# Weight sums of the first two feed-forward tiles on another engine, one shared slot, and a later place for the finishing of rows 0 to 3, in a transformer layer on one core

## The chip, the cores and the metric

The kernel runs on one core of a Trainium2 chip. The metric is the device time of one execution in microseconds, lower is better; several runs are given with their median.

## The reference, cut to what matters

One encoder layer: a mixing block with two attentions, a cross attention to 256 memory tokens, a SwiGLU feed-forward block, and a last RMSNorm. Sequence 1024, width 1024, inner width of the feed-forward block 2816, all float32. The change touches the feed-forward block and the last norm only:

```python
def rmsnorm(x, g):
    xf = x.astype(jnp.float32)
    y = xf * lax.rsqrt(jnp.mean(xf * xf, axis=-1, keepdims=True) + EPS)
    return (y * g.astype(jnp.float32)).astype(x.dtype)

def swiglu(h, w_gate_up, w_down):
    g, u = jnp.split(h @ w_gate_up, 2, axis=-1)
    return (jax.nn.silu(g) * u) @ w_down
...
        hf = rmsnorm(x, norm_ffn_g[layer])
        x = x + swiglu(hf, w_gate_up[layer], w_down[layer])
    return rmsnorm(x, norm_final_g)
```

## The kernel before, in words

Every product is a float32 product made of three matmuls on operands that are split into a high part (a cast on ScalarE, L896) and a low part (a subtraction on VectorE, L897): high by high, low by high, high by low (L902, L903, L904). The feed-forward block is class FeedForward. Both of its matrix products are done with seven sub-products instead of eight (a Strassen scheme), numbered 1 to 7 and taken in the order 1, 2, 6, 5, 7, 3, 4.

**First product (gate and up).** It goes over 11 tiles of 2 x 128 columns; Tile2 with f = 0 is here called tile 0, with f = 2 tile 1. Each tile has two pairs of weight blocks, g (gate) and u (up). A step of the list `items` is one sub-product of one pair: 12 matmuls of 128x512. The first 18 steps are: 1 g, 1 u, 2 g, 2 u of tile 0, the same four of tile 1, and then 6, 5, 7, 3, 4 (g and u each) of tile 0; steps 18 to 27 are 6, 5, 7, 3, 4 of tile 1. From tile 2 on, all seven follow one another.

- The weights of a pair are loaded into a tile `fr` with blocks a11, a12, a21, a22. Sub-products 6, 5, 7 and 3 need sums of blocks. Pair.make makes them in place on GpSimd, L956, L957, L958 (before 6) and L960 (before 3), each a tensor_tensor of 128x512. The sum s1 has a slot of its own of the kind "sum". make then splits the block into `w`. make is called four steps ahead (AHEAD).
- The activations (transposed, `hq`) are summed and split for each sub-product on VectorE and ScalarE by mov_late (L925, L927, L930, L935, then L897 into `T`); it is called in steps 2, 7, 9 and 11 for the sub-products 6 and 5, 7, 3 and 4.
- Pair.read takes results out of PSUM into rows `r`: L990 is the copy that opens a row (after 1, 6 and 5), L992 the addition of a later one. A PSUM bank of sub-product 1 takes 6 on top of it, so 6 of a pair cannot start before the copy after 1 of the same pair. What follows the products 1 and 2 of tile 1 is put off to step 15 (`later`).
- The slots: "sum" is a pool of two (tag raw), used for r of every u pair after sub-product 1 and for s1; "four" is a pool of eight (tag t2, 128x2048). Tile 1's g pair takes its row in half of a "four", its u pair in a "sum".
- At the end of sub-product 3 the gate row of tile 0 is multiplied by its up row (L1030, on VectorE for tile 0), which is the last use of u's row.

**Second product (down).** 77 steps, 11 for each of the seven sub-products, four row blocks (tt) of 12 matmuls / 4 each. down_make splits the operands two steps ahead into `do`; the last four go into other slots ("hidden"). `dr` are the loads, in a ring of eight: the load eight steps ahead waits for the split of the step that frees its slot, and stands in SyncE's queue in order. Sub-product 3 ends rows 0 to 3, sub-product 4 rows 4 to 7: add adds the PSUM bank (L1157), ScalarE takes squares (L1151), GpSimd makes the norm's factor (L1162 to L1164), and finish(row) scales both halves (L1145, VectorE) and sends them out (L1147, SyncE). Steps 72 to 76 of the list are done last, row block by row block.

The order of the instructions on each engine is drawn up at build time by a scheduler that takes the order of the code as priority and its own durations. `keep_in_program_order` (around L1145) pins an instruction behind the one that the code wrote before it on the same engine; nothing is pinned behind it. Each engine then works its list in order.

Of the kernel before, what the change touches and what calls it, by code (L numbers as in the profile page):

```python
# [12 lines left out]
ALU = mybir.AluOpType  # L13
# [10 lines left out]
FT = DFF // P  # L24
# [842 lines left out]
class FeedForward:  # L867
# [70 lines left out]
    class Pair:  # L938
# [11 lines left out]

        def make(self, n, w, s1):
            (a11, a12), (a21, a22) = ([self.raw[:, i, :HALF], self.raw[:, i, HALF:]] for i in range(2))
            pool, sub = self.ff.pool, ALU.subtract
            if n == 6:
                self.s1 = s1
                pool.tensor_tensor(out=s1, in0=a21, in1=a22, op=ALU.add)  # L956
                pool.tensor_tensor(out=a21, in0=a11, in1=a21, op=sub)  # L957
                pool.tensor_tensor(out=a11, in0=s1, in1=a11, op=sub)  # L958
            if n == 3:
                pool.tensor_tensor(out=a12, in0=a12, in1=a11, op=sub)  # L960
            src = {1: a11, 2: a12, 6: a11, 7: a21, 3: a12, 4: a22}[n] if n != 5 else self.s1
            self.w[n] = w
            self.ff.split(w[:, 0], w[:, 1], src)
# [13 lines left out]
        def read(self, n):  # L977
            ff = self.ff
            acc = self.bk[ff.BANK[n]]
            if n == 1:  # L980
                tile = ff.tiles["four"]("r")[:, :2] if self.f == 2 else ff.tiles["sum" if self.f >= FT else "row"]("r")
                self.r = [tile, None]
            elif n == 5:
                self.r[1] = ff.tiles["row"]("r")

            to = {1: (0, 0), 2: (0, 0), 6: (0, 1), 3: (0, 1), 5: (1, 1), 7: (1, 1)}.get(n)
            if to:
                r = self.r[to[0]][:, to[1]]
                if n in (1, 6, 5):
                    ff.act.copy(out=r, in_=acc)  # L990
                else:
                    ff.dve.tensor_tensor(out=r, in0=r, in1=acc, op=ALU.add)  # L992
# [139 lines left out]
    def down(self):  # L1132
        act, dve, pool, sp = self.act, self.dve, self.pool, self.sp
        LOADS, MADE, LAST = 8, 2, 5
        for i in range(4, LOADS):
            self.down_load(i)
        self.down_make(1)
        xs = []
        sf = self.cst.tile([P, NT, 2], F32, name="sf")
        bks = {}  # L1140
        fin = []

        def finish(row):
            for c in range(2):
                self.tc.keep_in_program_order(dve.scalar_tensor_tensor(  # L1145
                    out=xs[row][:, c], in0=xs[row][:, c], scalar=sf[:, row, 1:2], in1=gbc[:, c], op0=ALU.mult, op1=ALU.mult))
                sp.dma_start(out=self.out[row * P:(row + 1) * P, c * HALF:(c + 1) * HALF], in_=xs[row][:, c])  # L1147

        def squares(row, c):
            o = self.tiles["sum"]("fin")  # L1150
            act.activation(o[:, c], xs[row][:, c], AF.Square, accum_out=sf[:, row, c:c + 1])  # L1151

        def add(n, tt):
            b = "a" if self.BANK[n] == "a" else "c"
            half, c = {1: (0, 0), 2: (0, 0), 6: (0, 1), 5: (1, 1), 7: (1, 1), 3: (0, 1), 4: (1, 0)}[n]
            row = half * 4 + tt
            dve.tensor_tensor(out=xs[row][:, c], in0=xs[row][:, c], in1=bks[b][tt], op=ALU.add)  # L1157
            if n in (2, 7, 3, 4):
                squares(row, c)
            if n in (3, 4):  # L1160
                s0, s1 = sf[:, row, 0:1], sf[:, row, 1:2]
                pool.tensor_tensor(out=s1, in0=s0, in1=s1, op=ALU.add)  # L1162
                pool.tensor_scalar(out=s1, in0=s1, scalar1=1.0 / D, scalar2=EPS, op0=ALU.mult, op1=ALU.add)
                pool.tensor_tensor(out=s1, in0=s1, in1=self.mhalf, op=ALU.pow)  # L1164
                fin.append(row)
                if tt:
                    finish(fin[-2])
                if tt == 3:
                    finish(fin[-1])

        def mm(n, j, tt):
            bk = bks["a" if self.BANK[n] == "a" else "c"][tt]
            hi, lo = self.ops[self.ORDER.index(n) * (FT // 2) + j]
            ts = slice(tt * P, (tt + 1) * P)
            first = n in self.FIRST
            self.prod(bk, (hi[:, 0, ts], lo[:, 0, ts]), (hi[:, 1], lo[:, 1]), first and j == 0, j == FT // 2 - 1, not first)

        for i, (n, j) in enumerate(self.steps):
            if i >= len(self.steps) - LAST:
                break  # L1180
            self.down_load(i + LOADS)
            self.down_make(i + MADE)
            if i == 4:
                for x_d in self.x_d:
                    t = self.tiles["pair"]("xr")
                    sp.dma_start(out=t, in_=x_d)
                    xs += [t[:, k].rearrange("p (a b) -> p a b", a=2) for k in range(2)]
                gbc = self.tiles["row"]("gbc")
                sp.dma_start(out=gbc, in_=self.g_final.partition_broadcast(P).rearrange("p (a b) -> p a b", a=2))
            if n in self.FIRST and j == 0:  # L1190
                bks["a" if self.BANK[n] == "a" else "c"] = [self.bank() for _ in range(4)]
            for tt in range(4):
                mm(n, j, tt)
            if j == FT // 2 - 1:
                for tt in range(4):
                    add(n, tt)

        for k in range(i + MADE, len(self.steps)):
            self.down_make(k)
        for tt in range(4):  # L1200
            for n, j in self.steps[i:]:
                mm(n, j, tt)
            add(n, tt)
# [59 lines left out]
```

## Time and profile before

| what | us |
|---|---|
| median of 3 runs (lowest, highest) | 1790.8 (1789.49, 1791.02) |
| the profiled execution, its own time | 1787.65 |
| span of the profiled execution | 1785.8 |
| TensorE's mean granted clock, as a share of full speed | 0.997 |

All times in rows are from the start of the span of this one execution. The feed-forward block's first product starts at 1140.8, its second one at 1565. A row of the timeline gives start, duration, engine, line, operation, output and inputs, count of merged instructions, and in brackets how long the engine had been idle and what ended the idle time.

### The profile page before, as it was taken

Reading aid. Unit: us, or ns where it says so; the run is one execution under the profiler, and the core shown is the slowest. Engines: PE = TensorE matmul, PEld = TensorE weight load, DVE = VectorE, ACT = ScalarE, POOL = GpSimd, SP = SyncE. Lnnn points to the kernel's source line nnn. Section 1 sums busy time; section 2 is a strip of 40 time slices with the busy share of each in tenths; the row PEclk is TensorE's granted clock in tenths of the full one; section 3 lists DMA queues with packets and bytes.
Section 4 is the critical chain, followed back from the end, with each engine's and each line's share of the span. In section 5 each row is a group of like instructions: output and inputs, shape, how many; then the busy total and the mean of one; then the engine's idle time right before and its main releaser. Section 6 shows DMA issues by size and latency. Waiting matters only on the chain.

```text
span 1785.8 us, 23577 instructions
## 1 busy us (share of the span) xinstructions
PE 1743.1 (98%) x8836; PEld 1469.2 (82%) x8836; DVE 1085.4 (61%) x1497; ACT 765.6 (43%) x1425; POOL 516.0 (29%) x553
## 2 busy tenths in 40 slices
PE   7999999999999999999999999999999999999997
PEld 7778797898898888888888887778888888888886
DVE  6585666656766644435645545886676656655556
ACT  5354554545545544213542334453333333334343
POOL 3231213213323201200000001476766655400002
PEclk9999999999999999999999999999999999999999
DMA  5331313212222256412331113315645434587664
GB/s 193 103 93 66 102 47 104 65 60 61 68 85 63 76 195 233 156 62 86 116 118 49 58 59 135 125 71 195 253 163 191 165 142 174 215 283 193 195 192 139
DMA packets 75729, 229.79 MB, mean 129 GB/s; under 512 B 9184, under 2 KB 9440, under 8 KB 71776
## 3 DMA queue, kind: packets, MB, share of 16 engines
q1 hardware_dynamic: 75616, 228.30, 37.8%
q8 instruction: 69, 1.13, 0.3%
q14 instruction: 44, 0.36, 0.1%
HBM read 160.10 MB, written 55.57 MB: 121 GB/s over the span
## 4 chain that ended last, share of the span: by engine, by line
PE 65%; issue 3%; DVE 3%; ACT 1%; POOL 1%; DMA 1%; DVEq 0%; POOLq 0%; ACTq 0%
PE bk L903 11%; PE bk L904 11%; PE bk L902 11%; PE acc L217 5%; PE acc L218 5%; PE acc L219 5%; PE s L96 2%; PE s L95 2%; PE s L97 2%; PE s L217 2%; PE s L218 2%; PE s L219 2%; PE av L454 1%; PE tr L438 1%; PE av L95 0%
## 5 line engine op out<-in xcount | busy, mean ns | idle before, releaser
L218 PE MATMUL acc<-t,wsp 128*128 128x512 f32 (+1 forms) x704 | 270.5, 384 | 0.0
L217 PE MATMUL acc<-t,wsp 128*128 128x512 f32 (+1 forms) x704 | 270.5, 384 | 0.0
L219 PE MATMUL acc<-t,wsp 128*128 128x512 f32 (+1 forms) x704 | 270.4, 384 | 0.0
L902 PE MATMUL bk<-T,w 128*128 128x512 f32 x616 | 240.0, 390 | 2.2 <-ACT r L990 2.0
L903 PE MATMUL bk<-T,w 128*128 128x512 f32 x616 | 239.8, 389 | 1.3 <-DVE w L897 1.3
L904 PE MATMUL bk<-T,w 128*128 128x512 f32 x616 | 239.8, 389 | 0.4 <-DVE T L897 0.4
L897 DVE TENSOR_TENSOR w<-fr,w 128x512 fp32r<-128x512 f32 x132 | 142.9, 1115 | 69.5 <-ACT w L896 69.1
L81 DVE TENSOR_TENSOR wsp<-raw,wsp 128x1024 fp32r<-128x1024 f32 x98 | 122.1, 1246 | 74.1 <-ACT wsp L76 72.9
L76 ACT CAST wsp<-raw 128x1024 fp32r<-128x1024 f32 x96 | 100.7, 1049 | 124.8 <-PE s L219 50.2
L219 PEld LDWEIGHTS acc<-t,wsp 128*128 128x128 f32 x704 | 133.3, 189 | 25.2
L218 PEld LDWEIGHTS acc<-t,wsp 128*128 128x128 f32 x704 | 133.3, 189 | 23.0 <-DVE wsp L81 0.8
L217 PEld LDWEIGHTS acc<-t,wsp 128*128 128x128 f32 x704 | 133.3, 189 | 22.2
L897 DVE TENSOR_TENSOR do<-dr,do 128x1024 fp32r<-128x1024 f32 x77 | 96.5, 1260 | 78.3 <-ACT do L896 76.1
L902 PEld LDWEIGHTS bk<-T,w 128*128 128x128 f32 x616 | 115.6, 188 | 26.6 <-ACT r L990 2.4
L903 PEld LDWEIGHTS bk<-T,w 128*128 128x128 f32 x616 | 115.6, 188 | 25.5 <-DVE w L897 1.7
L904 PEld LDWEIGHTS bk<-T,w 128*128 128x128 f32 x616 | 115.6, 188 | 25.0 <-DVE T L897 0.9
L896 ACT CAST do<-dr 128x1024 fp32r<-128x1024 f32 x77 | 81.0, 1053 | 112.6 <-PE bk L904 98.6
L903 PE MATMUL bk<-do 128*128 128x512 f32 x308 | 120.0, 390 | 2.5 <-DVE do L897 2.5
L904 PE MATMUL bk<-do 128*128 128x512 f32 x308 | 119.8, 389 | 0.0
L217 PE MATMUL acc<-wsp,t 128*128 128x256 f32 (+1 forms) x368 | 118.3, 321 | 1.0 <-POOL wsp L80 1.0
L902 PE MATMUL bk<-do 128*128 128x512 f32 x308 | 119.0, 389 | 0.0
L219 PE MATMUL acc<-wsp,t 128*128 128x256 f32 (+1 forms) x368 | 116.8, 318 | 0.7 <-DVE wsp L81 0.7
(218 smaller groups left out, 3728.9 us busy)
## 6 DMA issues: line engine op xcount, KB each, us to landing
fr<-in_wgu SPq DMA_DIRECT2D x44, 512.0 KB, 5.3
ad<-r SPq DMA_DIRECT2D x22, 512.0 KB, 3.3
sd<-s SPq DMA_DIRECT2D x11, 1024.0 KB, 4.1
dw<-in_wdn SPq DMA_DIRECT2D x22, 512.0 KB, 5.4
wd<-dw SPq DMA_DIRECT2D x11, 1024.0 KB, 3.9
dr<-sd SPq DMA_DIRECT2D x44, 256.0 KB, 3.7
dr<-wd SPq DMA_DIRECT2D x44, 256.0 KB, 3.9
dr<-ad SPq DMA_DIRECT2D x33, 256.0 KB, 5.0
```

The source lines that it names most:

```text
L76: act.copy(out=hi, in_=src)
L81: lo_eng.tensor_tensor(out=lo, in0=src, in1=hi.bitcast(F32), op=ALU.subtract)
L95: pe.matmul(acc, lh, rh, start=(i == 0), stop=False)
L96: pe.matmul(acc, ll, rh, start=False, stop=False)
L217: pe.matmul(acc, lh, rh, start=(i == 0), stop=False)
L218: pe.matmul(acc, ll, rh, start=False, stop=False)
L219: pe.matmul(acc, lh, rl, start=False, stop=(i == n - 1))
L896: self.act.copy(out=hi, in_=src)
L897: self.dve.tensor_tensor(out=lo, in0=src, in1=hi.bitcast(F32), op=ALU.subtract)
L902: mm(acc, l[0], r[0], start=start, stop=False, skip_group_check=onto)
L903: mm(acc, l[1], r[0], start=False, stop=False, skip_group_check=onto)
L904: mm(acc, l[0], r[1], start=False, stop=stop, skip_group_check=onto)
```

## The change

The four kinds of weight sums of tiles 0 and 1 (both pairs) are issued on VectorE in place of GpSimd. The u pair of tile 1 takes its row in the second half of the "four" slot of its g pair, in place of a "sum" slot. The rows 0 to 3 are no longer finished at the end of sub-product 3, but one each after the steps j = 1, 2, 3, 4 of sub-product 4, the last one. Rows 4 to 7 are finished as before.

```diff
         def make(self, n, w, s1):
             (a11, a12), (a21, a22) = ([self.raw[:, i, :HALF], self.raw[:, i, HALF:]] for i in range(2))
-            pool, sub = self.ff.pool, ALU.subtract
+            sub = ALU.subtract
+            eng = self.ff.pool if self.f % FT >= 4 else self.ff.dve
             if n == 6:
                 self.s1 = s1
-                pool.tensor_tensor(out=s1, in0=a21, in1=a22, op=ALU.add)
-                pool.tensor_tensor(out=a21, in0=a11, in1=a21, op=sub)
-                pool.tensor_tensor(out=a11, in0=s1, in1=a11, op=sub)
+                eng.tensor_tensor(out=s1, in0=a21, in1=a22, op=ALU.add)
+                eng.tensor_tensor(out=a21, in0=a11, in1=a21, op=sub)
+                eng.tensor_tensor(out=a11, in0=s1, in1=a11, op=sub)
             if n == 3:
-                pool.tensor_tensor(out=a12, in0=a12, in1=a11, op=sub)
+                eng.tensor_tensor(out=a12, in0=a12, in1=a11, op=sub)
...
             if n == 1:
-                tile = ff.tiles["four"]("r")[:, :2] if self.f == 2 else ff.tiles["sum" if self.f >= FT else "row"]("r")
-                self.r = [tile, None]
+                if self.f % FT == 2:
+                    if self.f < FT:
+                        ff.second = ff.tiles["four"]("r")
+                    i = self.f // FT * 2
+                    self.r = [ff.second[:, i:i + 2], None]
+                else:
+                    self.r = [ff.tiles["sum" if self.f >= FT else "row"]("r"), None]
...
-        fin = []
...
-                fin.append(row)
-                if tt:
-                    finish(fin[-2])
-                if tt == 3:
-                    finish(fin[-1])
+                if n == 4 and tt:
+                    finish(row - 1)
+                if row == 7:
+                    finish(row)
...
             for tt in range(4):
                 mm(n, j, tt)
+            if n == 4 and j in (1, 2, 3, 4):
+                finish(j - 1)
```

## Rows read from the trace of the kernel before

**Rows 1.** The page's first part: busy time of each engine, share, instructions.
```profile
PE 1743.1 (98%) x8836; PEld 1469.2 (82%) x8836; DVE 1085.4 (61%) x1497; ACT 765.6 (43%) x1425; POOL 516.0 (29%) x553
```
**Rows 2.** TensorE's timeline from 1160: matmuls before which it sat idle.
```profile
1165.30 0.50 PE L903 MATMUL bk<-T,w 128*128 128x512 f32 x1 [1.27 <-DVE w L897]
...
1167.64 0.50 PE L904 MATMUL bk<-T,w 128*128 128x512 f32 x1 [0.45 <-DVE T L897]
...
1197.99 0.50 PE L902 MATMUL bk<-T,w 128*128 128x512 f32 x1 [1.96 <-ACT r L990]
...
1753.38 0.50 PE L903 MATMUL bk<-do 128*128 128x512 f32 x1 [2.03 <-DVE do L897]
...
1756.65 0.50 PE L903 MATMUL bk<-do 128*128 128x512 f32 x1 [0.48 <-DVE do L897]
```
**Rows 3.** GpSimd's timeline, 1143 to 1189: the weight sums of tiles 0 and 1.
```profile
1143.45 3.52 POOL L956 TENSOR_TENSOR s<-fr 128x512 f32<-128x512 f32 x2
...
1154.39 3.96 POOL L960 TENSOR_TENSOR fr<-fr 128x512 f32<-128x512 f32 x2
...
1170.60 13.72 POOL L956 TENSOR_TENSOR s<-fr 128x512 f32<-128x512 f32 x1 [12.25 <-ACT w L896]
...
1185.52 2.99 POOL L957 TENSOR_TENSOR fr<-fr 128x512 f32<-128x512 f32 x2
```
**Rows 4.** VectorE's timeline, 1138 to 1168.
```profile
1138.84 1.88 DVE L897 TENSOR_TENSOR w<-fr,w 128x512 fp32r<-128x512 f32 x3
...
1147.51 0.69 DVE L794 COPY hq<-bk 128x512 f32<-128x512 f32 x1 [1.68 <-PE bk L791]
1148.11 1.22 DVE L925 TENSOR_TENSOR hq<-hq 128x1024 f32<-128x1024 f32 x1
1149.75 1.28 DVE L897 TENSOR_TENSOR w<-fr,w 128x512 fp32r<-128x512 f32 x1 [0.42 <-ACT w L896]
1150.96 2.31 DVE L925 TENSOR_TENSOR hq<-hq 128x1024 f32<-128x1024 f32 x1
...
1155.43 1.77 DVE L897 TENSOR_TENSOR w<-fr,w 128x512 fp32r<-128x512 f32 x1
1157.12 2.31 DVE L927 TENSOR_TENSOR hq<-hq 128x1024 f32<-128x1024 f32 x1
...
1164.56 1.29 DVE L897 TENSOR_TENSOR w<-fr,w 128x512 fp32r<-128x512 f32 x2
...
1166.37 1.22 DVE L897 TENSOR_TENSOR T<-hq,T 128x1024 fp32r<-128x1024 f32 x1
```
**Rows 5.** Windows: length, busy time (instructions) of each engine, clock, DMA share, GB/s.
```profile
1170.00:1186.00 16.00, 16.00 (x72) 13.24 (x71) 15.90 (x19) 12.22 (x18) 15.40 (x3) 1.00 0.15 50
1186.00:1198.00 12.00, 10.04 (x46) 7.98 (x44) 6.49 (x9) 3.98 (x7) 8.95 (x7) 1.00 0.27 108
```
**Rows 6.** Timeline, 1196 to 1198, VectorE and ScalarE: what precedes the third idle time.
```profile
1196.10 1.22 DVE L1030 TENSOR_TENSOR r<-r 128x1024 f32<-128x1024 f32 x1
...
1197.35 0.59 ACT L990 COPY r<-bk 128x512 f32<-128x512 f32 x1 [1.37 <-DVE r L1030]
```
**Rows 7.** VectorE's timeline, 1743 to 1760: additions, finishing and splits.
```profile
1743.00 0.69 DVE L1157 TENSOR_TENSOR xr<-xr,bk 128x512 f32<-128x512 f32 x1 [1.09 <-PE bk L904]
...
1746.22 1.42 DVE L1145 SCALAR_TENSOR_TENSOR xr<-xr,sf,gbc 128x512 f32<-128x512 f32 x2 [0.80 <-POOL sf L1164]
...
1752.11 1.22 DVE L897 TENSOR_TENSOR do<-dr,do 128x1024 fp32r<-128x1024 f32 x1
...
1755.38 4.63 DVE L897 TENSOR_TENSOR do<-dr,do 128x1024 fp32r<-128x1024 f32 x4
```
**Rows 8.** TensorE's timeline at its end: the pace of matmuls without a wait.
```profile
1774.46 0.39 PE L902 MATMUL bk<-do 128*128 128x512 f32 x1
...
1777.63 0.39 PE L904 MATMUL bk<-do 128*128 128x512 f32 x1
```
**Rows 9.** SyncE's queue, 1747 to 1753: transfers out of the finished rows.
```profile
1747.00 5.55 SPq L1147 DMA_DIRECT2D out_dram<-xr  x6
```

## The prediction

> **What bounds the kernel now.** I read the page's busy times first: TensorE is busy 98% of the span, every other engine 61% or less [rows 1]. So time can only be won where TensorE sits idle, and the most that this change can win is the idle time in the parts that it touches. Next the timeline of TensorE from the start of the feed-forward block to the end: there are five idle times worth naming [rows 2]. Two stand at the sixth and last operand of step 8 (sub-product 6 of tile 0 is the first that needs sums): 1.27 us for the low part of `w` and 0.45 for the low part of `T`, both from VectorE. One of 1.96 waits for ScalarE's copy L990. Two, of 2.03 and 0.48, wait for a split in the first steps of sub-product 4, the last of the second product. That is 1.72 + 1.96 + 2.51 = 6.19 us. The matmul after each takes 0.50 in place of the 0.39 of a running stream [rows 2, 8], five times 0.11, so 0.55 more: 6.7 us is the ceiling. Between 1198 and 1753 TensorE has no such gap, so what is won before is kept to the end.
>
> Then I looked at who is late behind each of the five. For the first two, VectorE's timeline: from 1147.5 it has one idle time of 0.42 until step 8's operands are done, so step 8 waits for a queue that is full [rows 4]. While GpSimd works off tile 0's eight sums (1143.45 to 1158.35) [rows 3], VectorE's 128x1024 instructions take 2.31 in place of 1.22, and a 128x512 one 1.77 in place of 0.63 (1.88 for three) [rows 4]. The other way round, when VectorE is busy for 15.90 of 16 us [rows 5], one GpSimd sum takes 13.72 us, where two others take 2.99 together [rows 3]. The two slow each other. For the third idle time, the chain is a product L1030 on VectorE, the last use of the "sum" slot of tile 0's u row, which ends at 1197.3, and the copy of tile 1's u row, which starts at 1197.35 because it takes that slot, and TensorE starts when the copy's PSUM bank may be written again, at 1197.99 [rows 2, 6]. For the last two, VectorE had put splits behind the finishing of rows 0 to 3: one stands at 1752.11, after six L1145 [rows 7, 9].
>
> **The sums of tile 0.** The change takes eight instructions from GpSimd and puts eight on VectorE. One costs 1.88 / 3 = 0.63 us there (same shape, both inputs on chip) [rows 4]. Step 8 needs six of them (L956 to L958 for g and u), 3.8 us; the two L960 are needed at step 14 only and cost 1.3. What comes back: three 128x1024 instructions lose 1.09 each (first and last are shown), one 128x512 loses 1.1 and another, at 1.28, loses 0.65 [rows 4]: 5.0 us in all, on the queue that step 8 waits for. In addition VectorE sat idle 1.68 us before 1147.51 [rows 4], and tile 0's sums, which need nothing but a loaded weight, may fill that; whether they do is the scheduler's choice, which no row shows, so I keep 0 and 1.7 as bounds. The queue up to step 8 so gets shorter by 5.0 - 3.8 = 1.2, up to 2.9. The low part of `w` ended at about 1165.2 [rows 4] and is needed, without the stall, at 1165.30 - 1.27 = 1164.03: it comes at 1162.3 to 1164.0, in time. The low part of `T` ended at 1167.6 and is needed at 1167.64 - 0.45 - 1.27 = 1165.9: it comes at 1164.7 to 1166.4, between in time and 0.5 late. If the scheduler puts the L960 in front as well, it is 1.3 later still and 1.8 are lost, as before. I take 1.4 of the 1.72.
>
> **The sums of tile 1.** Another eight, 5.0 us, six of them before step 18. GpSimd had them done at about 1191.5 (L957 ends at 1188.5, two L958 at the same 1.5 follow) because its first one was held up for 13.72 us [rows 3]. VectorE is full until 1186, then busy 6.49 of 12 us [rows 5]: 5.5 us are free just there. With a queue that is at most 1.6 shorter by then (2.9 less the 1.3 of the L960), and at worst 0.1 longer, the six end between 1188 and 1190; cast and split of step 18 end some 1.3 later. Step 18 starts one step before the third stall, at 1197.99 - 1.96 - 2.72 = 1193.3, less the 1.4 won: 1191.9. (A step is 12 matmuls; 15 take 3.17 + 0.23 [rows 8], so 2.72.) So the cover is some 0.8 to 2.5 us of slack; should the sums be put ahead of the operands of steps 12 to 16, up to 1.0 is lost. I take 0.3 as the price.
>
> A rule speaks against moving this work here: the Trainium skill, Perfetto Trace Analysis, section Optimizing Scalar/DVE Operations, says that with VectorE saturated it may make sense to offload work to ScalarE or even GpSimd, and the change does the opposite on a VectorE that is full. The same section adds that between VectorE and GpSimd this might not help, because they share a read port; this trace agrees with that part, by 2.31 against 1.22 and 13.72 against 1.5. By the first half alone the 5.0 us would not come back and the sum would be that of the third rival below.
>
> **The slot.** Tile 1's u row lies beside the g row in a slot that the g row had anyhow, so no more slots are taken. Its copy no longer waits for L1030, and the bank is free long before step 19. The 1.96 go; what is late next is the weights of steps 18 and 19, priced above. The "sum" slots turn over earlier for tile 2, which nobody waits for.
>
> **The finishing.** Nothing is removed: eight L1145 of 0.71 (1.42 for two) and eight transfers move on by one to four steps. In the time from 1743.0 to the last split VectorE has four additions of about 0.63, ten splits of 1.16 (4.63 for four) and the eight L1145 [rows 7]: 2.5 + 11.6 + 5.7 = 19.8, so at the earliest they end at 1762.8. Now one step of 2.72 carries one split and one finish, 1.16 + 1.42 = 2.58: it fits. TensorE's last 60 matmuls start at 1777.63 + 0.23 - 60 x 0.2266 = 1764.3, without the stalls at 1761.6, and need the low part of the last split 13 matmuls later, at 1764.5. So VectorE may idle 1.7 us in this stretch; if it idles longer, one late split costs up to 1.16 at the end. On SyncE the six transfers that held its queue from 1747.00 to 1752.55, each behind its finish [rows 9], now stand behind the loads of later steps, so the last loads come sooner. The end (rows 4 to 7) is as before. Of the 2.51 I take 2.3.
>
> **The sum.** 1.4 + 1.96 + 2.3, less 0.3, is 5.4; with 0.4 of the restarts 5.8 us. The profiled execution, 1787.65, would be 1781.9, its span 1780.0. The median shown is 3.15 above the profiled execution; I take the 5.8 off the median: 1785.0 us.
>
> **The rivals.** *The stall of the last product moves* to the splits of the last five steps, since VectorE's 19.8 us barely fit: it costs 1.2 to 2.5 again, a gain of 3.3 to 4.6, 1786.2 to 1787.5. For it: the 1.7 us of slack against 1.9 us that VectorE idled in this stretch in two rows alone [rows 7]. Against: the four "hidden" splits have slots of their own and can fill gaps. *The slot gives nothing*: ScalarE's list keeps the copy behind the silu and products of tile 0 for the scheduler's reasons, and the 1.96 stay: gain 3.8, 1787.0. For it: only that ScalarE works in order; against: it idled 1.37 for the slot alone [rows 6]. *VectorE becomes the bound*: the slowing is not GpSimd's doing, or the sums are put in front of everything. Then step 8 comes 5.0 later, and if tile 1's 5.0 also stand in front of steps 12 to 16, about 3 more. Against the 4.5 of the other two parts that is +0.5 with tile 0's alone (1791.3, no change) and +3.5 with both (1794.3); it is slower than can be told from no change when more than 8.1 of the 10 us of sums land in front of TensorE. Against: GpSimd's sums and the slow VectorE rows coincide, and VectorE's rows are quick after 1158.
>
> **How the numbers follow.** A change of 0.2% (3.6 us) is about what a measurement of this kernel can tell from none; the three runs lie within 0.09%. Forecast 0.58, moved stall 0.12, slot without effect 0.10, VectorE's queue late by 2 to 5 us 0.13, by 8 or more 0.07. Faster: 0.53 + 0.06 + 0.05 + 0.03 = 0.67 (the moved stall and the slot rival straddle the 3.6); same: 0.05 + 0.06 + 0.05 + 0.10 = 0.26; slower: 0.07. The forecast's own range: all 6.7 and a run as low as the lowest shown (1.3) give 1783; at the worst of the bounds (0 at step 8, 1.0 lost at tile 1, one late split) 2.3 are won, 1788.5. The range 1783.2 to 1789.2 takes in the rivals but VectorE's later cases.
>
> **What would show it.** Right: GpSimd has no L956 to L960 before 1195; L925 and L927 at 1.22 all through; no idle time of TensorE above 0.6 at steps 8 and 19 and in sub-product 4; L990 for tile 1's u row before L1030. Wrong: TensorE idle behind VectorE's `w` or `T` at steps 8 to 18, or behind `do` in the last 60 matmuls.

## The result, and the profile after

| | median us (lowest to highest) | ratio to before on the same chip, 95% interval |
|---|---|---|
| kernel before, 6 runs | 1790.78 (1789.43 to 1791.02) | |
| changed kernel, 6 runs | 1780.67 (1779.73 to 1781.52) | 0.9945 [0.9933, 0.9958] |
| changed kernel on another chip | 1780.44, before 1789.36 | 0.9950 [0.9938, 0.9963] |

It is 10.1 us faster (8.9 on the second chip). 5.8 were forecast, 6.7 were called the ceiling, and 1780.67 lies below the range. The profiled execution of the changed kernel has a span of 1778.7 and a time of 1780.70, so the two profiles differ by 7.1 in span and the timed medians by 10.1.

The page of the changed kernel, first part:

```profile
PE 1741.4 (98%) x8836; PEld 1469.1 (83%) x8836; DVE 1088.3 (61%) x1513; ACT 766.1 (43%) x1425; POOL 481.6 (27%) x537
```

VectorE has 16 instructions more and GpSimd 16 fewer than in [rows 1]. TensorE's busy time by windows (length, busy time with its matmuls, clock, DMA share, GB/s), the stretches in which all five idle times of [rows 2] lay:

```profile
1163.00:1200.00 37.00, 37.00 (x163) 1.00 0.23 86
...
1740.00:1800.00 60.00, 31.19 (x138) 0.96 0.26 94
```

In the first no idle time is left. In the second there is none either until the last matmul at 1770.80 (below): the rest of that window is the end of the kernel. GpSimd's first sum, now one of tile 2, and VectorE's timeline at the first sums, which answers to [rows 3, 4] (L957 to L961 are the old L956 to L960):

```profile
1191.60 4.73 POOL L957 TENSOR_TENSOR s<-fr 128x512 f32<-128x512 f32 x2
```
```profile
1145.28 1.28 DVE L957 TENSOR_TENSOR s<-fr 128x512 f32<-128x512 f32 x2
1148.06 0.69 DVE L794 COPY hq<-bk 128x512 f32<-128x512 f32 x1 [1.49 <-PE bk L791]
...
1150.40 1.22 DVE L925 TENSOR_TENSOR hq<-hq 128x1024 f32<-128x1024 f32 x1
...
1152.67 0.69 DVE L897 TENSOR_TENSOR w<-fr,w 128x512 fp32r<-128x512 f32 x1
1153.27 1.22 DVE L927 TENSOR_TENSOR hq<-hq 128x1024 f32<-128x1024 f32 x1
...
1160.83 1.23 DVE L897 TENSOR_TENSOR T<-hq,T 128x1024 fp32r<-128x1024 f32 x1
1161.97 1.29 DVE L959 TENSOR_TENSOR fr<-s,fr 128x512 f32<-128x512 f32 x2
1163.18 1.22 DVE L930 TENSOR_TENSOR hq<-hq 128x1024 f32<-128x1024 f32 x1
1164.31 1.29 DVE L897 TENSOR_TENSOR w<-fr,w 128x512 fp32r<-128x512 f32 x2
...
1188.66 1.22 DVE L1036 TENSOR_TENSOR r<-r 128x1024 f32<-128x1024 f32 x1
```

The 128x1024 instructions take 1.22 where they took 2.31, and the 128x512 one 0.69 where one took 1.77. Two sums (L957) stand in front of the wait for the transposes. They fill little of its idle time, of which 1.49 is left of 1.68; their room comes from the instruction before them, which GpSimd's sums had slowed as well. Before, then after:

```profile
1143.52 2.31 DVE L110 SCALAR_TENSOR_TENSOR xn<-xs,rstd,gbc 128x1024 f32<-128x1024 f32 x1 [1.59 <-POOL rstd L103]
```
```profile
1144.08 1.28 DVE L110 SCALAR_TENSOR_TENSOR xn<-xs,rstd,gbc 128x1024 f32<-128x1024 f32 x1 [1.59 <-POOL rstd L103]
```

The feed-forward block starts at 1141.38 in this profile and at 1140.83 in the one before, so 0.55 has to be taken off when a place in it is compared. The last low part of T for step 8 ends at 1162.1 in place of 1167.6. The product that frees u's row (L1036, the old L1030) starts 7.4 us earlier. At step 8 TensorE's own order is another one too, with four high-by-high matmuls in a row, so that the low part of `w`, ready at 1165.0, is not waited for; in the old order it would have been needed some 0.4 earlier (1164.03 + 0.55 = 1164.6):

```profile
1164.19 1.32 PE L902 MATMUL bk<-T,w 128*128 128x512 f32 x4
1165.35 0.39 PE L903 MATMUL bk<-T,w 128*128 128x512 f32 x1
```

In the last product VectorE's timeline answers to [rows 7], SyncE's queue to [rows 9], TensorE's end to [rows 8]:

```profile
1746.37 1.41 DVE L1150 SCALAR_TENSOR_TENSOR xr<-xr,sf,gbc 128x512 f32<-128x512 f32 x2
1747.69 2.35 DVE L897 TENSOR_TENSOR do<-dr,do 128x1024 fp32r<-128x1024 f32 x2
...
1756.43 2.35 DVE L897 TENSOR_TENSOR do<-dr,do 128x1024 fp32r<-128x1024 f32 x2
```
```profile
1744.41 1.52 SPq L1130 DMA_DIRECT2D dr<-wd  x1
1747.14 18.99 SPq L1152 DMA_DIRECT2D out_dram<-xr  x9
```
```profile
1770.80 0.39 PE L904 MATMUL bk<-do 128*128 128x512 f32 x1
```

The finishes alternate with the splits, all loads are issued before the first transfer out, and the last split ends at 1758.8, before TensorE needs it (its last 60 matmuls start at 1770.80 + 0.23 - 13.6 = 1757.4, the low part of the last split is needed 2.9 later).

### The profile page after: what moved, and what is told of

Same layout as the page of the kernel before. It is cut to its first block, busy times and chain, and to the rows that moved or that the text cites. A ratio compares the mean times of both kernels' runs of the same rounds, so it can differ in the third digit from the quotient of the medians.

```text
span 1778.7 us, 23561 instructions
## 1 busy us (share of the span) xinstructions
PE 1741.4 (98%) x8836; PEld 1469.1 (83%) x8836; DVE 1088.3 (61%) x1513; ACT 766.1 (43%) x1425; POOL 481.6 (27%) x537
## 4 chain that ended last, share of the span: by engine, by line
PE 69%; ACT 1%; DVE 1%; issue 1%; POOL 0%; DVEq 0%; POOLq 0%; ACTq 0%
PE bk L902 12%; PE bk L903 12%; PE bk L904 12%; PE acc L217 5%; PE acc L218 5%; PE acc L219 5%; PE s L95 2%; PE s L97 2%; PE s L96 2%; PE s L217 2%; PE s L219 2%; PE s L218 2%; PE av L454 1%; PE tr L438 1%; PE av L95 0%
## 5 line engine op out<-in xcount | busy, mean ns | idle before, releaser
L902 PE MATMUL bk<-T,w 128*128 128x512 f32 x616 | 239.6, 390 | 0.2 <-ACT hq L794 0.2
L904 PE MATMUL bk<-T,w 128*128 128x512 f32 x616 | 239.7, 389 | 0.0
L902 PEld LDWEIGHTS bk<-T,w 128*128 128x128 f32 x616 | 115.6, 188 | 24.9 <-ACT hq L794 0.5
L904 PEld LDWEIGHTS bk<-T,w 128*128 128x128 f32 x616 | 115.6, 188 | 23.9
L902 PE MATMUL bk<-do 128*128 128x512 f32 x308 | 119.8, 389 | 0.0
L904 PE MATMUL bk<-do 128*128 128x512 f32 x308 | 119.8, 389 | 0.0
```

Source lines behind the costliest of these rows:

```text
L902: mm(acc, l[0], r[0], start=start, stop=False, skip_group_check=onto)
L904: mm(acc, l[0], r[1], start=False, stop=stop, skip_group_check=onto)
```

## The experiments

Two measures are used. The timed ratio has an interval of about 0.001 to each side, some 2 us. The *block length*, from the first L902 of step 0 to the last L904 in a profile, leaves out what happens before 1140 and is far finer: three profiles of kernels without idle time in it give 629.41, 629.42 and 629.43.

**The kernel before once more.**

> The kernel before once more, to see why its timed runs (1790.8) lie 3.1 us above its profiled execution (1787.65), while those of the changed kernel (1780.7) lie on theirs. Theory A (the touched places vary): in most executions the idle times of TensorE between 1160 and 1200 are some 3 us longer than in the profile that the prediction was made from, because GpSimd and VectorE hold each other up by a different amount each time; a profile of 1789 to 1791 then shows 9 to 10 us of idle time there and in the last product, in place of 6.2. Theory B (elsewhere): the same 6.2 us there, and the 3 us in stretches that the change does not touch. If the profile again has a span near 1786, it tells neither. The ratio is 1.000.

Timed 1788.26 against 1788.61 for itself, 0.9998 [0.9989, 1.0007]. Its profile has a span of 1788.8, 3.0 above the one that the prediction used, with nearly the same idle times (1.28, 0.46, 1.95, and 2.47 in one piece). TensorE's timeline and the windows of 1 us after the third of them:

```profile
1198.06 0.50 PE L902 MATMUL bk<-T,w 128*128 128x512 f32 x1 [1.95 <-ACT r L990]
...
1199.10 0.40 PE L903 MATMUL bk<-T,w 128*128 128x512 f32 x1
1199.32 0.60 PE L904 MATMUL bk<-T,w 128*128 128x512 f32 x1
1199.72 0.63 PE L902 MATMUL bk<-T,w 128*128 128x512 f32 x1
...
1755.51 0.64 PE L903 MATMUL bk<-do 128*128 128x512 f32 x1 [2.47 <-DVE do L897]
```
```profile
1198.00:1199.00 1.00, 0.94 (x4) 1.00 0.77 319
1199.00:1200.00 1.00, 1.00 (x5) 0.67 0.56 221
1200.00:1201.00 1.00, 1.00 (x3) 0.50 0.00 0
1201.00:1202.00 1.00, 1.00 (x4) 0.50 0.00 0
1202.00:1203.00 1.00, 1.00 (x5) 0.62 0.16 66
1203.00:1204.00 1.00, 1.00 (x6) 1.00 1.00 422
```

The number behind the bracketed count is the granted clock: 1.3 us after TensorE took up work again it falls from full speed to half, 2.4 to 1.2 GHz, and stays there for 3.4 us, in which the matmuls of a stream take 0.63 in place of 0.39 to 0.40. Another such stretch begins 0.2 us after the idle time of 2.47 that ends at 1755.5. Neither stretch is in the profile of [rows 2]. So theory A was right about the place and wrong about the mechanism: it is not the idle times that vary but what comes after them. From here on this is theory C; theory D says that an idle time costs its length.

**Three more profiles of the kernel before**, taken later for this question.

> The kernel before, one look. Theory C: half clock after none, one or both of the idle times at step 19 and in the last product, and a span near 1785.8 with none, 1.5 to 1.7 more with one, 3.0 with two (1788.8 was seen with two). Theory D: spans that differ by up to 4 us with the same clock after 1140.

> The kernel before, a second look: span against the number of half-clock stretches after 1140, as the look before it. If both kinds of place drop in most executions, the three looks hold three stretches or more.

> The kernel before, a third look, for the same comparison of span and half-clock stretches after 1140 as the two looks before it.

| profile of the kernel before | first L902 | last L904 | block length | half-clock stretches after 1140 |
|---|---|---|---|---|
| the prediction's | 1140.83 | 1777.63 | 636.80 | none |
| third of the three | 1142.18 | 1780.76 | 638.58 | one, after 1.96 |
| second of the three | 1142.70 | 1782.22 | 639.52 | two, after 1.90 and 2.26 |
| first of the three | 1140.14 | 1779.69 | 639.55 | two, after 1.90 and 2.34 |
| once more, above | 1140.89 | 1780.60 | 639.71 | two, after 1.95 and 2.47 |

The idle times are alike in all five (5.9 to 6.4 us together); the block length goes with the number of stretches, 1.4 to 1.8 us for each. With each profile's own idle times and 0.24 for each restart (worked out below) taken off, it is 1.6 for each stretch in all four. The prediction's profile is the only one of five without any.

**Each part alone.** The words behind # name the run and are not in the code.

```diff
+            eng = self.ff.pool if self.f % FT >= 4 else self.ff.dve   # sums only
...
+                if self.f % FT == 2:     # slot only
...
+            if n == 4 and j in (1, 2, 3, 4):     # finishing only
+                finish(j - 1)
```

> Only the sums of tiles 0 and 1 move to VectorE. By the sums of idle time the 1.27 and 0.45 at step 8 go (1.7 us, with restarts 1.9) and the 1.96 at step 19 stays, since the slot is as before. Theory A: the timed gain is 1.9 plus the 3.1 that only timed runs show, so about 5, 1786. Theory B: 1.9 in the timed runs too, 1789.

> Only the row of tile 1's u pair moves into the shared slot. The wait for the product L1030 goes: 1.96 plus 0.1. But the sums of tile 1 are still on GpSimd and held up, so step 18 or 19 may wait for them in its place, by 0 to 2 us. Theory A: 2 in the profile and up to 5 in the timed runs if the 3.1 sit in this wait; theory B: 0 to 2.1, 1789.

> Only the finishing of rows 0 to 3 moves. The two idle times in the last product go, 2.51 plus 0.2: 2.7 us, in the profile and in the timed runs, 1788.1. If the 3.1 that only timed runs show sit in the last product (transfers out in front of loads), the timed gain is near 5.8, 1785.

| kernel | ratio to before [interval] | us won | block length | idle times left, half-clock stretches in its profile |
|---|---|---|---|---|
| sums only | 0.9968 [0.9956, 0.9979] | 5.6 | 632.43 | 1.97, 0.43; none |
| slot only | 0.9986 [0.9978, 0.9995] | 2.5 | 635.62 | 1.27, 0.45, 2.27; one |
| finishing only | 0.9984 [0.9975, 0.9993] | 2.7 | 633.76 | 1.28, 0.46, 1.95; none |

The surprise is the first: the sums alone take away the third idle time too, although the slot is as before. In that kernel the product that frees u's row starts at 1187.64, as against 1196.10 in [rows 6], because VectorE's whole queue is earlier; the copy into the freed slot then comes in time, at 1188.89:

```profile
1187.64 1.21 DVE L1031 TENSOR_TENSOR r<-r 128x1024 f32<-128x1024 f32 x1
...
1188.89 0.59 ACT L991 COPY r<-bk 128x512 f32<-128x512 f32 x1
```

The gain of 5.6 is worked out, not shown, as 1.72 + 1.96, three restarts, and the stretch at half clock that four of the five profiles of the kernel before have after the third idle time. That theory A had put a gain of about 5 for this kernel is luck: it counted on the 1.96 to stay.

**Parts together.** The diff of the first is the change without the hunks on finish; that of the second the change without the hunk on make.

> The whole change but the finishing. If the slot adds something once the sums have moved, this is faster than the sums alone (0.9968 of before there). The profile of the sums alone showed no idle time at step 19 any more, so nothing is left for the slot: 0.9968, and the two idle times in the last product as before. If the slot's 2 us add to it: 0.9957.

> The slot and the finishing, with all sums on GpSimd as before. What stays is the 1.27 and 0.45 at step 8. If the parts add up: 2.5 + 2.7 = 5.2 us, 0.9971. By the idle times alone it would be all but 1.9 of the whole, so about 8, 0.9955; the first if the slot alone only moves the wait of step 19 to the sums of tile 1.

| kernel | ratio to before [interval] | us won | block length | idle times left, half-clock stretches in its profile |
|---|---|---|---|---|
| sums and slot | 0.9971 [0.9959, 0.9982] | 5.4 | 633.46 | 2.16; one |
| slot and finishing | 0.9961 [0.9949, 0.9974] | 6.4 | 631.48 | 1.27, 0.46; none |

Once the sums have moved, the slot adds nothing that can be seen (5.4 against 5.6). Without the sums, the slot does remove the wait, and the sums of tile 1, late on GpSimd, do not take its place. The 6.4 lies between the two sums expected. The sums with the finishing and without the slot, which by this would do as well as the whole change, were not run.

**Tile 1's sums back on GpSimd, and the sums of all tiles on VectorE.**

```diff
-            eng = self.ff.pool if self.f % FT >= 4 else self.ff.dve
+            eng = self.ff.pool if self.f % FT else self.ff.dve      # first run
...
-            eng = self.ff.pool if self.f % FT >= 4 else self.ff.dve
+            eng = self.ff.pool if False else self.ff.dve     # second run
```

> The whole change, but tile 1's sums stay on GpSimd. Step 8's idle times are gone if the slow VectorE there was due to tile 0's sums on GpSimd; tile 1's sums may again be held up by a full VectorE (a GpSimd sum of over 10 us in the profile) and step 18 or 19 wait for them, 0 to 3 us. Equal to the whole change (0.9945 to 0.995) if not.

> The whole change with the sums of all eleven tiles on VectorE, 88 in place of 16. The rival that VectorE becomes the bound: 72 more instructions of 0.63 are 45 us, on an engine that is busy some 60% of the first product; if it were late anywhere, TensorE idles before w. Otherwise equal to the whole change, since GpSimd's slowing of VectorE goes as well and TensorE has no gap there to lose.

The first: 0.9987 [0.9978, 0.9995], 2.5 us won, block length 635.27. It is worse than leaving all sums on GpSimd (6.4 won). Its waits of TensorE, and GpSimd's and VectorE's timelines:

```profile
PE bk L903 <- DVE w L897: 3.1, 2, 2.6
PE bk L902 <- ACT w L896: 0.3, 1, 0.3
```
```profile
1168.37 3.86 POOL L957 TENSOR_TENSOR s<-fr 128x512 f32<-128x512 f32 x2 [25.16 <-DVE w L897]
1172.19 4.49 POOL L958 TENSOR_TENSOR fr<-fr 128x512 f32<-128x512 f32 x2
```
```profile
1168.79 6.75 DVE L897 TENSOR_TENSOR T<-hq,T 128x1024 fp32r<-128x1024 f32 x3
...
1178.86 2.31 DVE L935 TENSOR_TENSOR hq<-hq 128x1024 f32<-128x1024 f32 x1
```

Here GpSimd starts tile 1's sums at 1168 and works them off at some 2 us each, and the slowing of [rows 4] is back, only ten microseconds later: three 128x1024 instructions take 6.75 in place of 3.50, and TensorE waits 2.55, 0.34 and 0.58 for operands of tile 0's last steps, with one stretch at half clock from the end of the 2.55 on. In the kernel before the same sums were held up by VectorE [rows 3], and TensorE waited for none of them. There GpSimd's and VectorE's timelines also show until when:

```profile
1170.60 14.97 POOL L956 TENSOR_TENSOR s<-fr 128x512 f32<-128x512 f32 x2 [12.25 <-ACT w L896]
```
```profile
1183.08 1.88 DVE L992 TENSOR_TENSOR r<-r,bk 128x512 f32<-128x512 f32 x3
```

The first of the two sums takes 13.72 and ends at 1184.32; the second, right behind it, takes 1.25. From 1170.60 on every instruction of VectorE has both inputs in SBUF, until the L992 at 1183.08, which reads one of them from a PSUM bank: the held-up sum ends 1.24 after that, its time when nothing holds it up. The Trainium skill, SBUF — State Buffer, section Who interferes with whom, states that a VectorE instruction with two inputs in SBUF and a GpSimd one that reads SBUF exclude each other, and that the order of issue decides which of them waits. These rows agree with the first half, 13.72 for a GpSimd sum there, 2.31 for VectorE here; they show that either engine can be the one that waits, but not by themselves why GpSimd gets its turn at 1168 here and not at 1170.60 there.

The second: 0.9952 [0.9938, 0.9965], block length 629.43, equal to the whole change. VectorE does not become the bound with 88 sums, and TensorE has nothing to lose to GpSimd in the later tiles.

**Idle times put in on purpose.** The changed kernel as a base, and three kernels with this before ten steps of the first product (k is 1, 3 and 4). The instruction adds zero times a PSUM bank, so nothing that is computed changes.

```diff
+                if i in range(40, 150, 12):
+                    _, q, m = self.items[i - 1]
+                    bank, hi = q.bk[self.BANK[m]], p.w[n][:, 0]
+                    for _ in range(k):
+                        self.dve.scalar_tensor_tensor(out=hi, in0=bank, scalar=0.0, in1=hi.bitcast(F32), op0=ALU.mult, op1=ALU.add)
                 p.mm(n)
```

> The changed kernel again, as the base for the three that follow on the same chip. Both theories: 0.9945 of before, some 1778.5 to 1780.7, no granted clock below full speed between 350 us and the end of TensorE's work.

> The changed kernel with ten idle times of TensorE put into the first product, one every 12 steps: one VectorE instruction, which adds zero times the PSUM bank of the step before to the high part of the weights, stands between two steps. By TensorE's and VectorE's rows at the end (a matmul's end, then an addition of 0.69 from PSUM) each is some 0.8 to 0.9 us. Theory D (an idle time costs its length): 10 x 0.9 + 10 x 0.1 for restarts, 9 to 10 us over the changed kernel. Theory C (an idle time may also bring a stretch of 3.4 us at half clock, 1.7 us more): the same here if idle times this short bring none, as those of 1.27 and 0.45 in the kernel before brought none in two profiles.

> The same ten places with three such instructions in a row, so idle times of some 2.0 us, the length of those before step 19 and in the last product of the kernel before. Theory D: 10 x 2.1, 21 us over the changed kernel, clock 0.997 as there. Theory C: in some of the places, from none in one execution to most in another, half clock follows; the profile shows such stretches right after idle times, and the timed excess is 21 plus 1.7 for each, some 25 to 35, with a granted clock of 0.990 to 0.995 in the mean.

> Four instructions in a row, idle times of some 2.6 us. Theory D: 27 us over the changed kernel. Theory C: half clock after most of them, 27 plus up to 17.

The lengths did not come out as meant: with its own order TensorE went on with other steps at most places, and the idle times are of all sizes. So the totals expected (9 to 10, 21 or 25 to 35, 27 or up to 44; timed 9.7, 23.3 and 28.3) do not decide between the theories, and the 9.7 of k = 1 fits only by luck. What follows each single idle time does.

| kernel | median us | block length over 629.41 | idle times in the block, us | half clock after |
|---|---|---|---|---|
| changed kernel again | 1780.44 | 0 | none | |
| k = 1 | 1790.14 | 9.8 | 0.35, 5.11 | 5.11 |
| k = 3 | 1803.71 | 23.9 | 0.22, 0.22, 0.76, 1.08, 1.83, 1.83, 2.49, 7.04 | one 1.83, 2.49, 7.04 |
| k = 4 | 1808.70 | 27.1 | 0.78, 2.16, 2.17, 2.50, 3.10, 8.86 | 2.50, 3.10, 8.86 |

The two idle times of 1.83 of k = 3, in TensorE's timeline and the windows after each:

```profile
1258.21 0.50 PE L902 MATMUL bk<-T,w 128*128 128x512 f32 x1 [1.83 <-DVE w L1110]
...
1506.24 0.50 PE L902 MATMUL bk<-T,w 128*128 128x512 f32 x1 [1.83 <-DVE w L1110]
```
```profile
1259.00:1260.00 1.00, 1.00 (x6) 1.00 0.93 352
1260.00:1261.00 1.00, 1.00 (x6) 1.00 0.80 328
...
1507.00:1508.00 1.00, 1.00 (x4) 0.69 0.88 332
1508.00:1509.00 1.00, 1.00 (x4) 0.50 0.86 344
```

The same length, once at full and once at half clock after it. Theory D misses: the idle times of k = 3 add up to 15.5, those of k = 4 to 19.6, and the block is 23.9 and 27.1 longer. With a restart of 0.24 each (below) and what the clock took while TensorE worked, summed over windows of 2 us (6.3, 5.2, and 3.0 for k = 1), theory C gives 23.7 and 26.2, and 8.9 of the 9.8 for k = 1; 0.2 to 0.9 are not explained. The 0.24 comes from two other profiles, so this is a test of it.

## Why the prediction was wrong, and what of it was right

**The step that failed** is the one that priced an idle time: "The matmul after each takes 0.50 in place of the 0.39 of a running stream [rows 2, 8], five times 0.11, so 0.55 more: 6.7 us is the ceiling." Two things are missing in it.

- *Half clock after an idle time.* The prediction put nothing for it. An idle time of TensorE of about 2 us is followed in some executions by 3.4 us at half clock, 1.6 us more. Over all profiles of this case after 1140: none after 1.3 us or less; after 1.8 to 2.3 us in eight of sixteen; after more than 2.3 us in all nine. The kernel before has two idle times of about that middle size (two of the ten are longer, 2.34 and 2.47), and five profiles of it show seven stretches of ten possible. The prediction's profile happened to show none. The Trainium skill, TensorE: Matmul & The Clock Gate, section HAM oscillation, tells that idle gaps between matmuls throw the clock back so that the next ones run slow; the runs here agree, and show it after shorter gaps than that section speaks of. At these lengths it changes from one execution to the next, why is not shown, and a single profile does not settle it.
- *The restart itself.* Between the prediction's profile and the changed kernel's, both at full clock, the block is 636.80 - 629.42 = 7.38 shorter, with 6.19 of idle time gone: 0.24 for each of five, not 0.11. The idle time is counted from the end of the last matmul, which is 0.39 long where the next would follow after 0.23; these 0.16 the prediction left out, and with its own 0.11 they make 0.27. The same difference in the three other profiles with idle times and no half clock in the block (sums only, finishing only, slot and finishing) gives 0.30, 0.22 and 0.17.

So between the two profiles alone the gain was 7.4 and not 5.8: the restarts are 1.2 where 0.4 were put, and all 6.19 of the idle time went where 5.4 were counted. The rest is the clock: the 5.8 should not have been taken off the median of the runs as they were. The prediction saw that this median lay 3.15 above the profiled execution and let it stand. Five block lengths of before average 638.8, so the mean gain in the block is 9.4; timed it was 8.9 and 10.1, each give or take some 2. The timed runs give no clock by place, but a mean for each run: 0.9966 over 15 runs of the kernel before and 0.9978 over five of the changed one on the second chip, 0.9969 over 16 of the kernel before and 0.9976 over five of the one with 88 sums on another chip. Over 1788 us that is some 2 to 4 us more at half clock in a run of the kernel before, so about one stretch. This is an estimate, and where in a timed run the stretches lie is not shown.

**Point by point.**

- *The sums of tile 0* (1.4 of 1.72 taken): all of it went, and VectorE's rows are quick again. The idle time of 1.68 was not filled; the room for two of the sums is the 1.03 that L110 no longer loses, which the prediction had not counted. T's low part came earlier than its bounds, at 1161.5 by the old block's time (1164.7 to 1166.4 given), but that of `w` later than its own, at 1164.4 (1162.3 to 1164.0 given), since two L959 and an L930 stand in front of it. That TensorE did not wait for it is owed to the four high-by-high matmuls that the scheduler put in front, which was not foreseen: here the forecast was lucky.
- *The sums of tile 1* (0.3 paid): the six were done at 1188.75, within the 1188 to 1190 given, and cost nothing. That leaving them on GpSimd after tile 0's had moved would bring 2.55 us of idle time at an earlier place was not seen; the part of the change that looked least needed guards the rest.
- *The slot* (1.96): the wait went, but the sums alone remove it too, since they bring L1030 forward. The two are not additive: for this wait one of them would have done.
- *The finishing* (2.3 of 2.51): both idle times went. VectorE ended its splits at 1758.8 with 1.6 us to spare; the slack had been put at 1.7.
- *The signs*: GpSimd's first sum comes at 1191.60, where none before 1195 was expected; the others came as written.
- *The rivals*: none came. VectorE as the bound is refuted by 88 sums in the same time. The rule of the Trainium skill that the prediction weighed (Perfetto Trace Analysis, section Optimizing Scalar/DVE Operations), that it may make sense to take work off a full VectorE, would have led the wrong way here: VectorE is now busy for 27.84 of the 28 us from 1170 to 1198, before it was for 22.39 [rows 5], and TensorE waits for nothing.

## What to carry to other kernels

An idle time of the bound engine costs more than its length: ask what the clock does after it, in several executions, before a ceiling is put up. Where timed runs lie above the profiled one by more than their spread, that difference belongs to something, and it has to be found before a gain is taken off the median. Work that slows a neighbour engine is priced by where it runs in time, and moving half of it can be worse than moving none.

## What the runs showed of the hardware that was not expected

- Half clock after idle times as short as 1.83 us, and not always: the same kernel, the same place and the same idle time (1.95 and 1.96) gave both.
- After idle times of 1.83 to 2.49 us the clock fell 0.1 to 1.4 us after work had begun again (1199.3 against 1198.06 above). With longer ones (2.50 to 8.86) it fell at the earliest 6.4 us before their end and at the latest 0.2 after it.
- A GpSimd sum of 128x512 took 1.25 us in one place and 13.72 us right before it, for as long as VectorE's instructions with both inputs in SBUF followed each other without a break. Which of the two engines is held up differed between two kernels in which GpSimd began 2.2 us apart.
